# Gate products moved to other stages, packed key weights and a longer turning lag in a two-layer attention trunk

## The chip, the cores and the metric

The kernel runs on one core of a Trainium2 chip. Its engines work beside each other: PE (TensorE, matrix products into PSUM), DVE (VectorE), ACT (ScalarE), POOL (GpSimd), and SP, whose queue here issues every DMA. The metric is the device time of one execution in microseconds (us); lower is better. The outputs must agree with the reference.

## The reference

Two layers of a trunk with 512 latent tokens and 256 context tokens of width 1024. In each layer one input projection feeds two attentions in parallel, a neighbourhood attention (A) and a grouped-query attention (B). Cut to what matters here:

```python
mod_x = jax.nn.silu(c) @ w_ada + b_ada
shift_x, scale_x, gate_x = jnp.split(mod_x[:, None, :], 3, axis=-1)
mod_c = jax.nn.silu(c_ctx) @ w_ada + b_ada
...
hx = _rmsnorm(x, norm_g) * (1.0 + scale_x) + shift_x
px = hx @ w_in
a_k, a_v, b_k, b_v, a_q, b_q, a_z, b_z, g_a, g_b = _split(px, SPLIT_SIZES)
...
a_att = _na_latent(qa, ka, va, cka, cva, rpb, rows)
...
qb = _rope_2d(_rmsnorm(hs(b_q, GQA_Q_HEADS), q_norm_b), pos_row, pos_col)
kb = _rope_2d(_rmsnorm(hs(b_k, GQA_KV_HEADS), k_norm_b), pos_row, pos_col)
b_att = _gqa_latent(qb, k_all, v_all)
out_x = _merge(a_att, b_att, a_z, b_z, g_a, g_b, w_o_a, w_o_b, w_out)
x_new = x + gate_x * out_x
```

`_merge` multiplies each attention by its SiLU path, projects it, weighs it by a sigmoid gate, adds both and projects again. The context tokens go through the same in layer 0; layer 1 needs only their keys and values. So `gate_x` (and `gate_c` in layer 0) is a product of a 1024-vector with the last third of `w_ada`, and it is used only at the end of a layer. It is the *residual gate* of the change.

## The kernel before

**Arithmetic.** Activations and weights are split into a rounded part and the rest (`hi` and `lo`, in fp32r), and each product is three products on PE (`mm3`, lines 346 to 348). A weight tile is loaded (SP) into one of three `raw` buffers, rounded on ACT into `whi`, and the rest is taken on POOL or DVE into `wlo`. `load_w` (line 309) does so one row tile of 128 rows at a time, and `load_w2` (line 323) packs two row tiles of 256 columns into one tile of 512. Both take their tiles from the pool `wp`, with eight `whi` and eight `wlo`, unless `own` names another pool. Token-major products (`tok_proj`) have the activations as weights of PE, channel-major ones (`chan_proj`) the weights.

**Stages of a layer.** First the keys of A (C_AK), values (C_AV) and queries (C_AQ); then A's attention; then keys and values of B (C_BKV) and its queries (C_BQ); then B's attention; then the merge and the output projection. `pipeline` (line 823) runs an attention over eight heads: the scores of head h, the values of head h - 1, and then some pieces of `fill`. The fill is a list of projections that belong to other parts (the SiLU paths, the sigmoid gates, branch A's output projection), in chunks of one weight load and its products; a load stands two chunks ahead of its products. In B's stage `run(fill, 2)` loads the first two chunks after the keys, and `PRE_GQ` pieces run right after the queries. `spread` says over how many heads the fill goes: 9 for A, 8 for B. In B all fill goes through the PSUM tile `psf`.

**Turning.** Keys and queries come token-major. They are normalised (squares on ACT, sums on DVE, the power on POOL), rotated (`rope_heads`, line 463, on DVE and POOL, result `rr`), and transposed on PE to channel-major. The transposes are put off: `to_channels` appends them to `hp["late"]`, and `tok_proj` turns all but the last `hp["lag"]` of them after each token tile. `after_products` (line 381) ties them to PE's place in program order.

**Gate products.** `ada_steps` (line 200) makes a list of steps: a broadcast of the conditioning vector's half into `cb`, and then for each of eight tiles of 128 gate channels a load of 256 KB into `rawb` (two buffers) and one DVE product and sum for the latent vector, in layer 0 a second one for the context vector (line 222, tiles `rawb` and `junk`). Each is tied to DVE's place in program order. There are two halves of the 1024 rows, and `ada_gate` adds them and sends the result out. Before the change the list of both halves runs in B's attention of the same layer: `pipeline` takes `att["per"]` steps after each score tile, two in layer 0 and one in layer 1. With `range(16)` the same helper makes the shifts and scales of layer 1 during layer 0, in the projections and in the output stage; that part stays as it is.

**Order.** The order on every engine's queue is fixed when the program is built. A scheduler follows program order as priority and a simulated timeline for readiness (`schedule_with_timeline_sim=True`), so instructions of neighbouring stages are interleaved. The probability tiles `p` are a ring of `NP_NA` or `NP_GQ` buffers.

Of the kernel before, what the change touches and what calls it, by code (L numbers as in the profile page):

```python
# [26 lines left out]
NP_GQ = (10, 10)  # L27
# [4 lines left out]
PRE_NA, PRE_GQ = 1, 2  # L32
XB, RX = 6, 2
# [14 lines left out]
def hybrid_kernel(es: ExitStack, tc, x, ctx, cvec, w_ada, w_ada0, small, gvec, w_in, w_o_a, w_o_b, w_out,  # L48
# [20 lines left out]
    pm = {}  # L69
# [130 lines left out]
    def ada_steps(l, tiles, halves, nv, pool):  # L200

        cb = {}

        def load(h):
            cb[h] = pool.tile([128, 2, 512], F32, tag="cb", name=nm("cb"), bufs=1)
            for v in range(nv):
                src = cd[8 * v + 4 * h:8 * v + 4 * h + 4].rearrange("k p -> (k p)").unsqueeze(0)
                nc.sync.dma_start(cb[h][:, v, :], src.to_broadcast([128, 512]))

        def load_tile(h, i):  # L210
            cb["w"] = pool.tile([128, 512], F32, tag="rawb", name=nm("rawb"), bufs=2)
            nc.sync.dma_start(cb["w"], w_ada[l, h, i])

        def dot(h, i, v):
            if v == 0:
                load_tile(h, i)
            w = cb["w"]
            o = w if v == nv - 1 else pool.tile([128, 512], BF16, tag="junk", name=nm("junk"), bufs=1)
            ins = nc.cur_bb.bb.instructions
            before = next(j for j in reversed(ins) if j.engine == mybir.EngineType.DVE)  # L220
            n = len(ins)
            V.tensor_tensor_reduce(o, w, cb[h][:, v, :], 1.0, 0.0, ALU.mult, ALU.add, asum[:, i, h, v:v + 1])
            for j in nc.cur_bb.bb.instructions[n:]:
                if j.engine == mybir.EngineType.DVE:
                    tc.add_manual_dep(j, before.name, mybir.DependencyInfo(
                        mybir.DependencyClass.NoSync, mybir.DependencyReason.DATA), reason="program order")
# [81 lines left out]
    def load_w(src, col0, n, nk, lo_eng, k0=0, own=None):  # L308

        pool, x = (wp, "") if own is None else (own, "x")  # L310
        res = []
        for k in range(k0, k0 + nk):
            raw = raw_tile()
            nc.sync.dma_start(raw[:, :n], src[128 * k:128 * k + 128, col0:col0 + n])
            hi = pool.tile([128, 512], F32R, tag="whi" + x, name=nm("whi"), bufs=8)
            S.copy(hi[:, :n], raw[:, :n])  # L316
            lo = pool.tile([128, 512], F32R, tag="wlo" + x, name=nm("wlo"), bufs=8)
# [63 lines left out]
    def after_products(fn):  # L381

        ins = nc.cur_bb.bb.instructions
        n, pe = len(ins), mybir.EngineType.PE
        last = next(i.name for i in ins[::-1] if i.engine == pe)
        fn()
        for i in nc.cur_bb.bb.instructions[n:]:
            if i.engine == pe:
                tc.add_manual_dep(i, last, mybir.DependencyInfo(
                    mybir.DependencyClass.NoSync, mybir.DependencyReason.DATA), reason="program order")  # L390
                last = i.name

    def turn_late(n):

        while len(hp["late"]) > n:
            after_products(hp["late"].pop(0))
# [67 lines left out]
    def rope_heads(npair, ps, rs, ta, tb, dst, t):  # L464
# [4 lines left out]
        r = hp["p"].tile([128, n], F32, tag=f"rr{npair}", name=nm("rr"), bufs=3)  # L469
# [11 lines left out]
    def layer(l, hx, nxt, mid):  # L481
# [5 lines left out]
        W = w_in[l]  # L487
        gq = gcol[:, 48 + 2 * l:49 + 2 * l]
# [114 lines left out]
        else:  # L603
# [4 lines left out]
            bg = []  # L608
# [26 lines left out]
        if True:  # L635
# [127 lines left out]
            def na_scores(h, q, kh, kl):  # L763
                load_bias(h)
                ps_ = []
                for i in range(4):
# [23 lines left out]
                    run(att["bg"], att["per"])  # L790
# [68 lines left out]
            pipeline(fill, 9, na_first, values_of(za, na_values))  # L859
# [7 lines left out]
            cosn = hp["p"].tile([128, 512], F32, tag="sq", name=nm("cosn"), bufs=2)  # L867
# [40 lines left out]
            for t in range(qt):  # L908
                tok_proj(w, 512, a_hx, t, evac_bq)
# [12 lines left out]
            def gq_scores(q, kh, kl):  # L922
                ps_ = []
                for i in range(4):
# [10 lines left out]
                    run(att["bg"], att["per"])  # L935
# [197 lines left out]
```

## Time and profile before

| | us |
|---|---|
| median of 3 runs | 1167.61 (1165.52 to 1169.21) |
| the profiled execution | 1166.55 |
| its span, first to last instruction | 1164.8 |
| granted TensorE clock, mean | 0.997 |

The stages by the trace of the profiled execution: layer 0 starts A's attention at about 140 us, B's keys at 306, B's attention at 375, the merge at 570; layer 1 begins its projections at about 700, A's attention at 780, B's keys at 882, B's attention at 955 and the merge at 1100.

In the profile a line such as "L222 DVE ... rawb<-rawb,cb ... x64 | 53.8, 841" is a group of instructions of one source line, engine and tile: 64 of them, 53.8 us in all, 841 ns on average. Behind the second bar stands the idle time of the engine before them and what ended it. A row of a stretch gives the busy time of each engine in it with the number of instructions, then the granted clock, and DMA's share and rate; for one tile it counts only instructions that write or read this tile. PE's matrix instructions overlap, so their shown durations are longer than the step from one to the next.

### The profile page before, as it was taken

How to read it: one execution, taken by the hardware profiler on the slowest of the kernel's cores; microseconds unless marked ns; L12 is line 12 of the kernel's file. 1: busy time of each engine (PE TensorE's matmuls, PEld its weight loads, DVE VectorE, ACT ScalarE, POOL GpSimd, SP SyncE). 2: the span in 40 equal slices, each digit the busy share in tenths (PEclk: the TensorE clock that was granted, in tenths of full speed). 3: DMA queues.
4: the chain of work that ended last, by engine and by line, in shares of the span. 5: the costliest groups of instructions: out<-in, count | busy, mean ns of one | idle time of the engine just before them, and what ended most of it. 6: DMA issues, size and time to landing. Idle time of an engine off the chain costs nothing.

```text
span 1164.8 us, 17332 instructions
## 1 busy us (share of the span) xinstructions
PE 1127.1 (97%) x6078; PEld 948.9 (81%) x6078; DVE 812.0 (70%) x1512; ACT 574.3 (49%) x1175; POOL 498.0 (43%) x463
## 2 busy tenths in 40 slices
PE   5999999999999999999999999999999999999998
PEld 4688888988988888888788787888888878877686
DVE  4556588876364799798588755349877757898573
ACT  5452266665343555666431355337665445756531
POOL 3362354443275334353411227345544664645311
PEclk9999999999999999999999999999999999999999
DMA  9534212221351343461434423403322525452133
GB/s 372 200 110 136 71 46 65 84 83 63 111 164 47 115 134 100 81 259 37 139 133 123 151 71 92 126 25 107 104 74 66 171 90 182 142 176 91 37 132 95
DMA packets 88129, 134.05 MB, mean 115 GB/s; under 512 B 10757, under 2 KB 52713, under 8 KB 86377
## 3 DMA queue, kind: packets, MB, share of 16 engines
q1 hardware_dynamic: 88040, 132.94, 35.3%
q8 instruction: 48, 0.79, 0.3%
q14 instruction: 41, 0.33, 0.1%
HBM read 115.58 MB, written 17.32 MB: 114 GB/s over the span
## 4 chain that ended last, share of the span: by engine, by line
PE 72%; DVE 10%; POOL 6%; issue 4%; DMA 3%; ACT 2%; SPq 0%; ACTq 0%; POOLq 0%; DVEq 0%
PE psx L348 10%; PE psx L346 10%; PE psx L347 10%; PE psf L346 8%; PE psf L347 8%; PE psf L348 8%; PE pst L654 4%; PE pss L703 2%; PE pss L704 2%; PE pss L780 2%; POOL rsb L255 2%; DVE ptl L658 2%; DMA rawb<-in_w_ada_dram 1%; PE psv L948 1%; DVE mx L930 1%
## 5 line engine op out<-in xcount | busy, mean ns | idle before, releaser
L658 DVE TENSOR_TENSOR ptl<-pst,pth 128x512 fp32r<-128x512 f32 (+1 forms) x176 | 116.1, 671 | 41.0 <-ACT pth L657 40.0
L657 ACT CAST pth<-pst 128x512 fp32r<-128x512 f32 (+1 forms) x176 | 98.9, 576 | 91.7 <-PE pst L654 63.3
L346 PE MATMUL psf<-hx,whi 128*128 128x512 f32 (+1 forms) x368 | 139.4, 379 | 0.0
L347 PE MATMUL psf<-hx,whi 128*128 128x512 f32 (+1 forms) x368 | 138.3, 376 | 0.0
L348 PE MATMUL psf<-hx,wlo 128*128 128x512 f32 (+1 forms) x368 | 138.2, 375 | 0.0
L333 POOL TENSOR_TENSOR wlo<-raw,whi 128x512 fp32r<-128x512 f32 x64 | 91.0, 1425 | 109.9 <-ACT whi L331 96.5
L346 PE MATMUL psx<-whi,hx 128*128 128x512 f32 (+1 forms) x368 | 136.9, 373 | 0.0
L347 PE MATMUL psx<-wlo,hx 128*128 128x512 f32 (+1 forms) x368 | 136.2, 370 | 0.0
L348 PE MATMUL psx<-whi,hx 128*128 128x512 f32 (+1 forms) x368 | 133.8, 370 | 0.0
L319 POOL TENSOR_TENSOR wlo<-raw,whi 128x512 fp32r<-128x512 f32 (+1 forms) x52 | 67.4, 1296 | 149.6 <-ACT whi L316 132.0
L316 ACT CAST whi<-raw 128x512 fp32r<-128x512 f32 (+1 forms) x112 | 65.2, 592 | 112.6 <-PE psx L348 38.3
L331 ACT CAST whi<-raw 128x512 fp32r<-128x512 f32 x128 | 77.6, 621 | 53.2 <-DMA raw<-in_w_in_dram 39.6
L654 PE MATMUL pst<-ident,p 128*128 128x128 f32 x640 | 100.6, 273 | 1.7 <-DVE ptl L658 1.2
L654 PEld LDWEIGHTS pst<-ident,p 128*128 128x128 f32 x640 | 78.1, 141 | 13.7 <-DVE ptl L658 1.0
L644 POOL TENSOR_TENSOR p<-p,r 128x512 f32<-128x512 f32 (+1 forms) x64 | 85.7, 1339 | 5.2
L333 DVE TENSOR_TENSOR wlo<-raw,whi 128x512 fp32r<-128x512 f32 x64 | 62.7, 980 | 31.0 <-ACT whi L331 30.6
L319 DVE TENSOR_TENSOR wlo<-raw,whi 128x512 fp32r<-128x512 f32 (+1 forms) x60 | 48.2, 807 | 45.9 <-ACT whi L316 45.6
L643 POOL TENSOR_SCALAR r<-r 128x1 f32<-128x1 f32 x64 | 21.5, 336 | 137.1 <-DVE r L638 126.6
L346 PEld LDWEIGHTS psx<-whi,hx 128*128 128x128 f32 x368 | 69.8, 190 | 11.9 <-issue 0.8
L348 PEld LDWEIGHTS psf<-hx,wlo 128*128 128x128 f32 x368 | 69.4, 189 | 11.9
L348 PEld LDWEIGHTS psx<-whi,hx 128*128 128x128 f32 x368 | 69.6, 189 | 11.3
L346 PEld LDWEIGHTS psf<-hx,whi 128*128 128x128 f32 x368 | 69.5, 189 | 11.1 <-ACT zt L502 0.3
(239 smaller groups left out, 3065.8 us busy)
## 6 DMA issues: line engine op xcount, KB each, us to landing
raw<-in_w_in_dram SPq DMA_DIRECT2D x160, 256.0 KB, 2.9
rawb<-in_w_ada_dram SPq DMA_DIRECT2D x64, 256.0 KB, 2.7
gs<-zt SPq DMA_DIRECT2D x32, 256.0 KB, 2.4
raw<-in_w_out_dram SPq DMA_DIRECT2D x32, 256.0 KB, 2.8
tg<-gs SPq DMA_DIRECT2D x4, 1536.0 KB, 8.6
rawx<-in_w_ada_dram SPq DMA_DIRECT2D x4, 1024.0 KB, 6.4
rawy<-in_w_ada_dram SPq DMA_DIRECT2D x4, 1024.0 KB, 12.2
raw<-in_w_o_a_dram SPq DMA_DIRECT2D x16, 256.0 KB, 3.3
```

The lines of the kernel that those rows point to most:

```text
L255: G.tensor_tensor(b[:, :w], a[:, :w], ehalf[:, :w], ALU.pow)
L316: S.copy(hi[:, :n], raw[:, :n])
L319: e.tensor_tensor(lo[:, :n], raw[:, :n], F(hi[:, :n]), ALU.subtract)
L331: S.copy(hi, raw)
L333: lo_eng(i).tensor_tensor(lo, raw, F(hi), ALU.subtract)
L346: T.matmul(ps, lhs[0], rhs[0], start=first, stop=False)
L347: T.matmul(ps, lhs[0], rhs[1], start=False, stop=False)
L348: T.matmul(ps, lhs[1], rhs[0], start=False, stop=last)
L644: G.tensor_tensor(p[:, c0:c1], p[:, c0:c1], r[:, i:i + 1].to_broadcast([128, c1 - c0]), ALU.mult)
L654: T.transpose(pt[:, c0:c0 + 128], src, ident)
L657: S.copy(hi[:, n0:n1], pt[:, n0:n1])
L658: V.tensor_tensor(lo[:, n0:n1], pt[:, n0:n1], F(hi[:, n0:n1]), ALU.subtract)
```

## The change

The gate products leave B's attention in part. In layer 0 the first half goes to A's attention, one step a score tile from head 4 on, and the second half stays in B's, one step a score tile. In layer 1 both halves go to the projections of A. B's key and value weights are loaded packed, two row tiles a tile. B's query weights are loaded ahead of B's key products; four of the eight row tiles come from `wp` and four from B's own pool with four buffers. The keys' transposes lag three token tiles instead of two, and the ring of rotated keys has four tiles. The rotation tables of the keys are made first and those of the queries behind the fourth key tile. The cosine tile gets a buffer of its own, and layer 1's B has 11 probability tiles instead of 10. `behind` is `after_products` for any engine.

```diff
-NP_GQ = (10, 10)
+NP_GQ = (10, 11)
...
-    def load_w(src, col0, n, nk, lo_eng, k0=0, own=None):
+    def load_w(src, col0, n, nk, lo_eng, k0=0, own=None, bufs=8):
...
-    def after_products(fn):
+    def behind(engine, fn):
...
-        r = hp["p"].tile([128, n], F32, tag=f"rr{npair}", name=nm("rr"), bufs=3)
+        r = hp["p"].tile([128, n], F32, tag=f"rr{npair}", name=nm("rr"), bufs=4 if npair == 1 else 3)
...
+        nv = 2 if first else 1
+
+        def gate_steps(halves, pool):
+            return (ada_steps(l, range(16, 24), halves, nv, pool)
+                    + ([lambda: ada_gate(l, nv)] if 1 in halves else []))
...
-            bg = []
+            bg = gate_steps((0, 1), hp["p"])
+            run(bg, 1)
         per_bg = -(-len(bg) // (2 + qt))
...
-                    run(att["bg"], att["per"])
+                    run(att["bg"], 1)
...
                 n = len(fill)
-                att["bg"], att["per"] = bg, -(-len(bg) // 30)
                 prev = None
                 for h in range(8):
+                    att["bg"] = bg if h > 3 or pm["n"] == 1 else []
...
-            pipeline(fill, 9, na_first, values_of(za, na_values))
+            bg = gate_steps((0,), att["p"]) if first else []
+            pipeline(fill, 9, na_first, values_of(za, na_values), bg=bg)
...
-            cosn = hp["p"].tile([128, 512], F32, tag="sq", name=nm("cosn"), bufs=2)
+            cosn = hp["p"].tile([128, 512], F32, tag="cosn", name=nm("cosn"), bufs=1)
...
-            for i in range(2):
+
+            def make_tabs(i):
...
+            make_tabs(1)
...
-            w = load_w(W, C_BKV, 256, KT, mix_lo)
+            bg = []
+            w = load_w2(W, C_BKV, KT, mix_lo)
+            w_q = load_w(W, C_BQ, 512, 4, bq_lo) + load_w(W, C_BQ, 512, 4, bq_lo, 4, hp["p"], 4)
+            hp["lag"] = 3
             for t in range(6):
                 tok_proj(w, 256, a_hx, t, evac_bkv)
+                if t == 3:
+                    behind(ON_DVE, lambda: make_tabs(0))
+                run(bg, 1)
+            hp["lag"] = 2
             qbv = big("qb").rearrange("p (j n) -> p j n", j=4)
-            w = load_w(W, C_BQ, 512, KT, bq_lo, own=hp["p"])
...
-                tok_proj(w, 512, a_hx, t, evac_bq)
+                tok_proj(w_q, 512, a_hx, t, evac_bq)
+                run(bg, 2)
...
-            nv = 2 if first else 1
-            bg = ada_steps(l, range(16, 24), (0, 1), nv, att["p"]) + [lambda: ada_gate(l, nv)]
-            run(bg, 1)
+            bg = gate_steps((1,), att["p"]) if first else []
             pipeline(fill, 8, gq_first, values_of(zb, gq_values), early, bg)
```

In the stages of B's keys and queries `bg` is empty, so the two `run(bg, ...)` there do nothing.

More of the change, by code (lines that the diff above doesn't have):

```diff
@@ L32 @@
 PRE_NA, PRE_GQ = 1, 2
+ON_PE, ON_DVE = mybir.EngineType.PE, mybir.EngineType.DVE
 XB, RX = 6, 2
@@ L218, in dot @@
             o = w if v == nv - 1 else pool.tile([128, 512], BF16, tag="junk", name=nm("junk"), bufs=1)
[L219 to L226, printed above, removed]
+            behind(ON_DVE, lambda: V.tensor_tensor_reduce(o, w, cb[h][:, v, :], 1.0, 0.0, ALU.mult, ALU.add,
+                                                          asum[:, i, h, v:v + 1]))
         res = []
@@ L314, in load_w @@
             nc.sync.dma_start(raw[:, :n], src[128 * k:128 * k + 128, col0:col0 + n])
-            hi = pool.tile([128, 512], F32R, tag="whi" + x, name=nm("whi"), bufs=8)
+            hi = pool.tile([128, 512], F32R, tag="whi" + x, name=nm("whi"), bufs=bufs)
             S.copy(hi[:, :n], raw[:, :n])
-            lo = pool.tile([128, 512], F32R, tag="wlo" + x, name=nm("wlo"), bufs=8)
+            lo = pool.tile([128, 512], F32R, tag="wlo" + x, name=nm("wlo"), bufs=bufs)
             e = lo_eng(k)
@@ L379, in hybrid_kernel @@
     hp = {"late": [], "lag": 0}
-    def after_products(fn):
+    def behind(engine, fn):
         ins = nc.cur_bb.bb.instructions
-        n, pe = len(ins), mybir.EngineType.PE
-        last = next(i.name for i in ins[::-1] if i.engine == pe)
+        n = len(ins)
+        last = next(i.name for i in ins[::-1] if i.engine == engine)
         fn()
         for i in nc.cur_bb.bb.instructions[n:]:
-            if i.engine == pe:
+            if i.engine == engine:
                 tc.add_manual_dep(i, last, mybir.DependencyInfo(
@@ L395, in turn_late @@
         while len(hp["late"]) > n:
-            after_products(hp["late"].pop(0))
+            behind(ON_PE, hp["late"].pop(0))
     def run(fill, n):
```

2 lines of the change are left out of this document (1 added, 1 removed).

## The prediction

> **What bounds the kernel now.** I read the profile's first lines, then the busy time of each engine by stage, then, for the stages that the change touches, the same table for single tiles.
>
> ```profile
> PE 1127.1 (97%) x6078; PEld 948.9 (81%) x6078; DVE 812.0 (70%) x1512; ACT 574.3 (49%) x1175; POOL 498.0 (43%) x463
> ```
>
> PE is busy for 1127.1 of 1164.8 us. The change takes no product from PE, so it can give only time that PE now loses: 37.7 us that show as idle, and some more inside the modelled ends. Where that lies, stage by stage:
>
> ```profile
> core 0: us, PE busy (x) PEld busy (x) DVE busy (x) ACT busy (x) POOL busy (x), PEclk, DMA share, GB/s
> 80.00:140.00 60.00, 60.00 (x280) 49.47 (x280) 38.78 (x88) 15.95 (x27) 21.73 (x19) 1.00 0.35 106
> 140.00:225.00 85.00, 85.00 (x529) 75.89 (x528) 71.21 (x142) 54.80 (x117) 43.18 (x38) 1.00 0.21 63
> 225.00:300.00 75.00, 75.00 (x475) 67.06 (x474) 49.65 (x107) 42.41 (x100) 26.62 (x30) 1.00 0.21 69
> 390.00:475.00 85.00, 83.69 (x500) 72.64 (x498) 79.49 (x157) 47.64 (x103) 31.85 (x28) 1.00 0.36 115
> 475.00:580.00 105.00, 100.75 (x616) 87.38 (x615) 77.80 (x133) 59.22 (x120) 51.04 (x42) 1.00 0.39 124
> 700.00:780.00 80.00, 78.93 (x366) 64.67 (x365) 34.68 (x52) 35.20 (x64) 38.80 (x34) 1.00 0.28 85
> 880.00:898.00 18.00, 16.57 (x114) 13.91 (x113) 12.22 (x28) 11.22 (x24) 5.86 (x7) 1.00 0.20 63
> 920.00:955.00 35.00, 31.69 (x145) 25.16 (x144) 19.66 (x24) 13.37 (x25) 23.75 (x18) 1.00 0.30 92
> 955.00:1035.00 80.00, 78.63 (x396) 65.26 (x396) 65.16 (x119) 47.94 (x93) 40.70 (x33) 1.00 0.60 195
> 1035.00:1060.00 25.00, 25.00 (x135) 21.00 (x134) 21.06 (x35) 16.22 (x32) 10.10 (x10) 1.00 0.29 85
> 1060.00:1100.00 40.00, 36.16 (x190) 26.79 (x189) 28.23 (x47) 24.12 (x47) 18.41 (x18) 1.00 0.12 41
> ```
>
> In order: projections of layer 0 (80 to 140); its first attention (140 to 225 early heads, 225 to 300 late heads); its second attention (390 to 475, with the gate products, and 475 to 580); projections of layer 1 (700 to 780); the end of its first attention (880 to 898); the queries of its second (920 to 955); that attention itself (from 955). The late part of layer 0's first attention leaves DVE idle for a third, while the start of its second keeps DVE busy for 79.49 of 85 and PE loses 1.31. Layer 1 loses 3.31 in 920 to 955, 1.37 in 955 to 1035 and at least 3.84 in 1060 to 1100.
>
> How much that last stretch really loses I count. First the steps from start to start of queued PE instructions:
>
> ```profile
> 301.17 0.40 PE L346 MATMUL psf<-hx,whi 128*128 128x512 f32 x1
> 301.40 0.39 PE L347 MATMUL psf<-hx,whi 128*128 128x512 f32 x1
> ...
> 891.03 0.27 PE L652 MATMUL pst<-ident,p 128*128 128x128 f32 x1
> 891.14 0.49 PE L654 MATMUL pst<-ident,p 128*128 128x128 f32 x3
> ```
>
> So a 512-wide product takes 0.23 and a transpose 0.11, whatever their shown durations. Next, for the same stretch, the rows of the tiles psf, pst, psv, pss and psx in this order:
>
> ```profile
> 1060.00:1100.00 40.00, 3.60 (x12) 1.71 (x10) 0.66 (x1) 0.00 (x0) 1.00 0.12 41
> ...
> 1060.00:1100.00 40.00, 13.11 (x88) 10.75 (x88) 14.91 (x23) 12.70 (x22) 1.00 0.12 41
> ...
> 1060.00:1100.00 40.00, 18.71 (x48) 8.65 (x48) 2.74 (x4) 2.32 (x4) 1.00 0.12 41
> ...
> 1060.00:1100.00 40.00, 5.38 (x24) 4.02 (x24) 5.66 (x6) 6.15 (x14) 1.00 0.12 41
> ...
> 1060.00:1100.00 40.00, 3.99 (x18) 3.48 (x19) 0.00 (x0) 0.00 (x0) 1.00 0.12 41
> ```
>
> 88 transposes x 0.11 + 102 products x 0.23 = 33.2, so 6.8 of the 40 us are lost. Only 12 of these products are fill (psf): the projections that are put between attention steps have run out, and PE follows DVE and ACT. The attention's progress is the DVE count of tile ptl, six a head:
>
> ```profile
> 955.00:1035.00 80.00, 6.69 (x16) 3.02 (x16) 10.71 (x16) 1.00 0.60 195
> 1035.00:1060.00 25.00, 3.16 (x8) 1.51 (x8) 6.89 (x10) 1.00 0.29 85
> 1060.00:1100.00 40.00, 10.75 (x24) 4.50 (x24) 14.91 (x23) 1.00 0.12 41
> ```
>
> When the fill ends at 1060, 26 of 49 are done (48, and one counted at a border). **The attention lags its fill**, and the gate products (lines 222) stand in DVE in the part where it falls behind.
>
> **The change part by part.**
>
> ```profile
> L222 DVE CUSTOM_DVE_ANT_0 rawb<-rawb,cb 128x512 f32<-128x512 f32 x64 | 53.8, 841 | 1.5 <-DMA rawb<-in_w_ada_dram 0.8
> L222 DVE CUSTOM_DVE_ANT_0 junk<-rawb,cb 128x512 bf16<-128x512 f32 x48 | 37.0, 772 | 9.9 <-DMA rawb<-in_w_ada_dram 9.6
> ...
> L222 DVE DVE_READ_ACCUMULATOR2_ANT asum<- 128x1 f32 x112 | 9.0, 80 | 0.0
> ```
>
> *Layer 1's gate products leave its second attention.* 16 x (0.841 + 0.080) = 14.7 us of DVE, 16 loads and two broadcasts go. Without them DVE needs 65.16 - 14.7 + 21.06 + 28.23 = 99.75 for 49 steps, 2.04 each, so 14.7 us are worth 7.2 steps. At the fill's end 33 instead of 26 would be done; the tail shrinks from 23 steps to 16, and its 6.8 with it: -2.1. Of the 1.37 before it I take half: -0.7. Together **-2.8**. Bounds: 0 if DVE does not pace the attention (it is at 81%, not full), -8.2 if the fill then lasts to the end.
>
> *They go to layer 1's projections*, 16 products in six tile steps. DVE there has 34.68 of 80, with them 49.4, or 62%. The nearest row is layer 0's same stage, 80 to 140, which holds 32 such products at 38.78 of 60 (65%) with PE busy for 60.00 of 60.00. Cost **0**; cover gone, 14.7.
>
> ```profile
> SPq L212 <- DVE asum L222: 105.0, 48, 11.6
> ...
> PE pst L422 <- DVE rr L477: 4.1, 7, 1.4
> ```
>
> Their loads pass SP, where a load waits for one of two buffers, up to 11.6 us, with the weights of the next projection behind it. In layer 0 that happened under a full PE too, so it stays at nothing. The gate sum and its small transfer come some 300 us before their use.
>
> *Layer 0's first half goes from the second attention to heads 4 to 7 of the first.* It takes 8 x (0.841 + 0.772) + 16 x 0.080 = 14.2 from DVE. In 390 to 475 DVE falls from 94% to 77%, and I give back the idle time of that stretch: **-1.3**; bounds 0 and -3.4, the last if half of the 4.25 lost in 475 to 580 goes as well. The second half now comes one step a score tile, through five heads. At its new place DVE rises from 49.65 to 63.9 of 75, 85%. The nearest row, 140 to 225, has 84% and no PE idle, so **0**. The other bound is the bare end of layer 1's first attention, where fill is gone: by the share of weight loads in a full stretch (67.06 of 75) the 13.91 there are 15.6 us of work in 18, so +2.4. Eight loads and two broadcasts stand there before bias loads and weights in SP; the same cover holds.
>
> *Packing, early query weights, third lag.*
>
> ```profile
> raw<-in_w_in_dram SPq DMA_DIRECT2D x160, 256.0 KB, 2.9
> ...
> raw<-in_w_in_dram SPq DMA_DIRECT2D x16, 128.0 KB, 2.1
> ```
>
> Eight 128 KB transfers a layer become four of 256 KB: 16.8 us of landings become 11.6, and the casts halve in number and double in width. PE does the previous stage meanwhile: nothing, and at most 5.2 a layer gained. The slots matter more. Four of eight query weight pairs now use the shared eight, and keep them until the last query product. So only the first of the two prefetched fill chunks can load during the queries. Layer 1 shows what the second one does there now, in the chain of waits, on ACT, and on PE:
>
> ```profile
> 918.03 4.69 DMA raw<-in_w_in_dram
> ...
> 922.75 0.62 ACT whi L331
> ```
> ```profile
> 922.75 1.25 ACT L331 CAST whi<-raw 128x512 fp32r<-128x512 f32 x2 [2.47 <-DMA raw<-in_w_in_dram]
> 923.90 0.60 ACT L404 ACTIVATE sq<-psf 128x512 f32<-128x512 f32 x1
> ...
> 932.47 0.63 PE L422 MATMUL pst<-ident,rr 128*128 128x128 f32 x4 [1.41 <-DVE rr L477]
> ```
>
> The squares of the first query tile queue on ACT behind a cast that waits for a fill weight, and at the end PE waits 1.41 for the rotated queries. Of the 4.1 in seven such waits of both layers I take this one and 0.1 of the keys' own: **-1.5**. Bounds: -4.1, and the second chunk too late, which is a rival. Next late is then POOL's chain for the later query tiles, at 23.75 of 35. The eleventh probability tile lets scores run one tile further ahead and the two later tables take two DVE instructions off the front: nothing.
>
> Sum: -2.8 + 0 - 1.3 + 0 - 1.5 = **-5.6** on the profiled execution's 1166.55 (span 1164.8 and 1.75 around it), or 1160.95. The median of the runs, 1167.61, stands 1.06 higher; I add half to every case: **1161.5**.
>
> [...]
>
> ```profile
> L222 DVE CUSTOM_DVE_ANT_0 rawb<-rawb,cb x64: 667/691/1889, 92.5 to 1030.4; 128x512 f32<-128x512 f32 x64
> ```
>
> Some of them take 1.889 where the median is 0.691, so they meet something. If each of the 16 in layer 1 held POOL's chain of the norms by 0.69, and PE with it, that were +11.0. [...]
>
> **The rivals.**
>
> *More: the fill lasts.* The whole 6.8 and 1.37 of layer 1, 3.4 of layer 0 and the 1.5 go: -13.1, 1154.0. For it: PE loses nothing in 1035 to 1060, where fill is there. Against it: the last head's values come behind all fill.
>
> *Nothing but the queries.* The order on each engine is set when the program is built, and already puts query weights and fill early. If the attention is paced by the chain of PE, ACT and DVE and not by DVE's sum, only -1.5 is left: 1165.6. For it: DVE at 81% in 955 to 1035; against it: 94% in layer 0.
>
> *Slower: the second fill chunk is late.* It cannot load before the last query product.
>
> ```profile
> L331 ACT CAST whi<-raw 128x512 fp32r<-128x512 f32 x128 | 77.6, 621 | 53.2 <-DMA raw<-in_w_in_dram 39.6 <-PE psf L347 4.8 <-PE psx L347 3.5
> ...
> L333 POOL TENSOR_TENSOR wlo<-raw,whi 128x512 fp32r<-128x512 f32 x64 | 91.0, 1425 | 109.9 <-ACT whi L331 96.5 <-PE psx L347 10.1 <-PE psf L347 2.6
> ```
>
> One tile takes 2.9 + 0.62 + 1.43 = 4.95, four in a row 19.8. Against it stand the first chunk's products, 48 x 0.23 = 11.0 in layer 1, and half as much again, 16.5, in layer 0. If nothing overlaps, PE waits 8.8 and 3.3, and the query gain is gone: -4.1 + 12.1 = +8.0, 1175.1. It decides once the four take over 11.0 together; with three buffers they should overlap to some 9.
>
> *Slower: POOL held by the moved products*, as above: -5.6 + 11.0, 1172.5.
>
> **How the numbers follow.** The forecast gets 0.50, more gain 0.15, the queries alone 0.20, the late chunk 0.10, POOL held 0.03; 0.02 is for what I don't see. About 0.3%, 3.5 us, can be told from no change here, so faster means under 1164.1. The forecast (own range 1158.5 to 1164.5) puts 0.48 there, the larger gain 0.15 and the queries alone 0.02: 0.65. Within: 0.22, mostly the queries alone. Slower: 0.13. The range goes from just below the larger gain, 1153.5, to 1170, and leaves out the two slower cases.
>
> **What would show it.** Right: no line-222 work after 955; the ptl count before the fill's end in layer 1 over 30; PE in the last 40 us before its merge above 36.16; DVE in the first 85 us of layer 0's second attention near 65 and PE full; PE still full in late layer 0 heads; no wait of over 1 us for rotated queries in layer 1. Wrong: the tail keeps its 23 steps (DVE did not pace it), PE waits for fill weights right after the queries (slots), or layer 0's first attention ends bare.

## The result and the profile after

The changed kernel takes 1155.68 us (median of 4 runs, 1154.87 to 1157.16) against 1166.57 for the kernel before, run beside it (4 runs, 1165.51 to 1169.21). The ratio is 0.9905, 95% interval 0.9883 to 0.9926, so it is 11.1 us faster, give or take 2.5. The forecast's sum was 5.6. The profiled execution has a span of 1153.4 against 1164.8.

The first row of the page of after, busy time of each engine, and the table by stage, cut at the borders that correspond to those of before (columns as there):

```profile
PE 1123.0 (97%) x6078; PEld 949.0 (82%) x6078; DVE 809.8 (70%) x1508; ACT 573.9 (50%) x1167; POOL 495.0 (43%) x459
```

```profile
80.00:140.00 60.00, 60.00 (x281) 49.44 (x280) 38.87 (x88) 15.93 (x27) 21.21 (x20) 1.00 0.37 106
225.00:300.00 75.00, 74.65 (x471) 66.60 (x470) 59.85 (x137) 42.23 (x98) 31.83 (x30) 1.00 0.34 103
389.00:474.00 85.00, 84.78 (x516) 74.75 (x516) 65.54 (x126) 48.87 (x104) 30.66 (x28) 1.00 0.27 87
474.00:570.00 96.00, 91.70 (x562) 79.17 (x561) 73.71 (x125) 56.61 (x115) 46.07 (x39) 1.00 0.36 107
700.00:776.00 76.00, 75.25 (x350) 61.59 (x349) 41.24 (x84) 32.57 (x56) 38.70 (x34) 1.00 0.49 137
876.00:894.00 18.00, 16.54 (x111) 13.83 (x110) 13.85 (x30) 11.36 (x24) 6.34 (x7) 1.00 0.23 64
916.00:946.00 30.00, 30.00 (x141) 24.58 (x140) 20.42 (x22) 13.38 (x24) 23.88 (x18) 1.00 0.33 101
946.00:1026.00 80.00, 80.00 (x412) 66.99 (x411) 58.32 (x92) 53.11 (x103) 38.05 (x35) 1.00 0.38 130
1048.00:1088.00 40.00, 37.23 (x194) 28.62 (x193) 28.02 (x44) 22.55 (x42) 17.05 (x15) 1.00 0.18 54
```

The reader is to see four things. Layer 1's queries (916 to 946) now keep PE full, where 920 to 955 before had 31.69 of 35. The attention behind them (946 to 1026) has PE full too, and its last 40 us hold 37.23 against 36.16. The start of layer 0's second attention (389 to 474) has DVE at 65.54 of 85, where it had 79.49, and PE at 84.78 against 83.69. Layer 0's late first heads (225 to 300) took the gate products and lose 0.35.

PE issues the same 6078 matrix instructions in both kernels, so the gain must be time that PE lost between them. I count it by stage: from the start of each PE instruction to the start of the next, less the step of a queued one (0.228 and 0.120 us for 512 and 256 columns, the usual steps inside the stretches where PE is full, and 0.082 for 128, the mean over a burst of three transposes, whose steps are 0.109, 0.109 and 0.028). A stage reaches from its attention's first query split (tile `qs` on DVE) to its last head's output (`ho`), or from that to the next `qs`. This is my own sum over the trace's rows. Its level hangs on the steps taken, its differences hardly do. One trace of each kernel stands behind it, and traces scatter: in `e1_gates`, `e2_gates_l1` and `e7_defer`, experiments below that leave the order of ScalarE in this stage as before has it, layer 1's keys and queries lose 4.3, 5.4 and 4.2, so that the 5.4 of before stands at the upper end and some 1 us in this row is no effect of the change.

| lost by PE, us | before | after |
|---|---|---|
| layer 0: up to its first attention | 18.0 | 18.3 |
| layer 0: first attention | 6.2 | 6.7 |
| layer 0: keys and queries of the second | 2.7 | 1.3 |
| layer 0: second attention | 17.2 | 15.1 |
| layer 0's output and layer 1's projections | 5.5 | 4.8 |
| layer 1: first attention | 9.4 | 9.4 |
| layer 1: keys and queries of the second | 5.4 | 1.0 |
| layer 1: second attention | 17.0 | 13.6 |
| layer 1: output | -0.4 | -0.4 |
| sum | 81.1 | 69.7 |

The difference, 11.4, is the whole difference of the spans. The keys' and queries' stages of both layers give 5.8 of it, the two second attentions 5.5.

### The profile page after: what moved, and what is told of

Read it like the earlier page. It is cut to its first block, busy times and chain, and to the rows that moved or that the text cites. A ratio compares the mean times of both kernels' runs of the same rounds, so it can differ in the third digit from the quotient of the medians.

```text
span 1153.4 us, 17280 instructions
## 1 busy us (share of the span) xinstructions
PE 1123.0 (97%) x6078; PEld 949.0 (82%) x6078; DVE 809.8 (70%) x1508; ACT 573.9 (50%) x1167; POOL 495.0 (43%) x459
## 4 chain that ended last, share of the span: by engine, by line
PE 83%; DVE 7%; issue 3%; POOL 2%; ACT 2%; DMA 2%; ACTq 0%; POOLq 0%; DVEq 0%
PE psx L341 12%; PE psx L343 12%; PE psx L342 12%; PE psf L341 9%; PE psf L342 9%; PE psf L343 9%; PE pst L655 5%; PE pss L704 2%; PE pss L705 2%; PE psv L959 2%; PE psv L958 1%; PE pss L781 1%; PE pst L417 1%; DVE wlo L328 1%; DVE ptl L659 1%
## 5 line engine op out<-in xcount | busy, mean ns | idle before, releaser
L328 POOL TENSOR_TENSOR wlo<-raw,whi 128x512 fp32r<-128x512 f32 x68 | 95.0, 1402 | 108.9 <-ACT whi L326 87.8
L314 POOL TENSOR_TENSOR wlo<-raw,whi 128x512 fp32r<-128x512 f32 x44 | 60.4, 1373 | 140.4 <-ACT whi L311 123.8
L311 ACT CAST whi<-raw 128x512 fp32r<-128x512 f32 x96 | 58.7, 623 | 103.5 <-PE psx L343 38.6
L326 ACT CAST whi<-raw 128x512 fp32r<-128x512 f32 x136 | 82.5, 622 | 50.3 <-DMA raw<-in_w_in_dram 34.1
L328 DVE TENSOR_TENSOR wlo<-raw,whi 128x512 fp32r<-128x512 f32 x68 | 70.2, 1033 | 28.3 <-ACT whi L326 27.8
L342 PEld LDWEIGHTS psx<-wlo,hx 128*128 128x128 f32 x368 | 69.6, 189 | 11.0
```

Source lines behind the costliest of these rows:

```text
L326: S.copy(hi, raw)
L328: lo_eng(i).tensor_tensor(lo, raw, F(hi), ALU.subtract)
L342: T.matmul(ps, lhs[0], rhs[1], start=False, stop=False)
```

## The experiments

All ratios are to the kernel before, run beside the kernel, with 95% intervals.

### The gate products alone

`e1_gates` is before with all moves of the gate products, `e2_gates_l1` with those of layer 1 alone. Both have `gate_steps` and the new place in layer 1's projections; the first also has `run(att["bg"], 1)` and the new place in layer 0's first attention. In the second:

```diff
-            bg = []
+            bg = gate_steps((0, 1), hp["p"])
+            run(bg, 1)
         per_bg = -(-len(bg) // (2 + qt))
...
-            bg = ada_steps(l, range(16, 24), (0, 1), nv, att["p"]) + [lambda: ada_gate(l, nv)]
+            bg = gate_steps((0, 1), att["p"]) if first else []
```

> The kernel before with only the gate products moved (both layers). By the recorded reasons: -2.8 in layer 1's second attention and -1.3 in layer 0's, so -4.1 us against the kernel before, ratio 0.9965. By a second reading, from the two traces (unbroken steps of PE counted stage by stage): some -5.5, ratio 0.995. By the rival that DVE does not pace the attention: 0, ratio 1.000. If layer 0's first attention ends bare, its late heads lose PE time.

> The kernel before with only layer 1's gate products moved to its projections; layer 0's stay. By the recorded reasons -2.8 us, ratio 0.9976, with the ptl count at the fill's end near 33; by the second reading -3.4, ratio 0.997; by the rival 0.

Measured: all moves 1161.78, ratio 0.9960 (0.9947 to 0.9973), layer 1's alone 1163.46, 0.9981 (0.9972 to 0.9989). So layer 1's move is worth about 2.2 us by the ratio, and layer 0's 2.4 more by the ratios or 1.7 by the medians; the intervals are about as wide as that difference. The count agrees: in `e2_gates_l1` layer 1's second attention loses 14.5 instead of 17.0, in `e1_gates` layer 0's loses 14.9 instead of 17.2 and its first attention 6.8 instead of 6.2. Layer 1's second attention of `e2_gates_l1`, all tiles (the first stretch is 955 to 1035, as before):

```profile
955.00:1035.00 80.00, 79.88 (x409) 66.76 (x408) 57.84 (x90) 52.52 (x103) 37.19 (x34) 1.00 0.39 132
1060.00:1100.00 40.00, 36.52 (x188) 27.43 (x187) 24.82 (x40) 23.00 (x43) 17.43 (x16) 1.00 0.13 41
```

Before, the same stretches had PE at 78.63 and 36.16 and DVE at 65.16. The DVE count of the tile ptl, which says how far the attention has come when its fill ends, goes from 26 steps of 48 before to 30 in both kernels. What the prediction said of the gate products holds in mechanism and roughly in size.

### The keys' and queries' stage alone, and what of it is needed

`e3_keys` is the change without the moves of the gate products and with 10 probability tiles. It has the packing, the query weights loaded ahead of the key products and split over two sets of slots, the longer lag, the fourth `rr` tile, the cosine tile's own buffer and the later tables. From there parts are taken back. `e4_keys_own8` gives all eight query weight pairs slots of their own, and `e5_keys_small` keeps the split; both have lag 2, three `rr` tiles and the cosine tile in its old buffer. `e6_keys_late` is `e3_keys` with the loads behind the key products in program order. `e4_keys_own8` differs from `e3_keys` in these lines, besides the `rr` tiles and the cosine tile:

```diff
-            w_q = load_w(W, C_BQ, 512, 4, bq_lo) + load_w(W, C_BQ, 512, 4, bq_lo, 4, hp["p"], 4)
-            hp["lag"] = 3
+            w_q = load_w(W, C_BQ, 512, KT, bq_lo, own=hp["p"])
...
-            hp["lag"] = 2
```

> The changed kernel with the gate products put back where they were and 10 probability tiles: only the stage of the second attention's keys and queries is changed. By the recorded reasons -1.5 us, ratio 0.9987. By the second reading, that this term was undersized, -5.5, ratio 0.9953, most of it in layer 1 between its first and second attention.

> As e3_keys, but all eight query weight pairs in the stage's own pool, so that the second fill chunk can load during the queries again (for its room the cosine tile shares a buffer as before, three tiles of rotated keys, lag 2). Slots theory (the gain is that the second chunk's casts no longer stand ahead of the query squares on ACT): at most -2 us, ratio over 0.998, with PE waiting over 1 us for rotated queries in layer 1. Early-weights theory (the gain comes from the query weights' place): the same as e3_keys within 1 us. Lag theory (three tiles against two): over 1 us slower than e3_keys, with waits at the keys' transposes.

> The same as e4_keys_own8 but with the four and four split of the change: it differs from e4 only in the slots. Slots theory: some 3 to 4 us faster than e4, ratio 0.996 to the kernel before. Early-weights theory: equal to e4. Lag theory: equal to e4, both slower than e3_keys.

> As e3_keys, but the query weights (four and four) are loaded after the keys' products in program order, as before. Early-weights theory: loses most of e3's gain, ratio over 0.998. Slots theory: keeps it, within 1 us of e3_keys.

Measured: `e3_keys` 1161.62, 0.9963 (0.9951 to 0.9975); `e4_keys_own8` 1163.39, 0.9973 (0.9963 to 0.9983); `e5_keys_small` 1161.41, 0.9959 (0.9947 to 0.9972); `e6_keys_late` 1162.13, 0.9975 (0.9966 to 0.9984). The stage alone is worth 4.3, not 1.5. Without lag, fourth tile and cosine buffer it is worth as much, so these do nothing that can be measured. The place of the loads in program order does not show in layer 1's stage either: it loses 1.0 in `e3_keys`, `e5_keys_small` and `e6_keys_late` alike, though 3.0 in `e4_keys_own8`. (The time of `e6_keys_late` gains less than that of `e3_keys`, 2.9 against 4.3, but the intervals overlap, and what the count shows of it is 0.3 in layer 1's second attention.) The slots matter, though less than all of the gain: 1.6 lie between `e4_keys_own8` and `e5_keys_small`, which differ in nothing else, and 3.1 are left without the split, more than the 1.6 that the packing gives alone (next section). So without the split the early place may be worth something. In both comparisons the intervals overlap.

Why shows in ScalarE's and GpSimd's timelines of layer 1 (start, duration, and behind the shape the idle time before it). First before: the square of the first key tile, one of the casts behind it, and GpSimd's first and last instruction for the query tiles:

```profile
898.39 0.27 ACT L404 ACTIVATE sq<-psf 128x128 f32<-128x128 f32 x1
...
911.37 0.62 ACT L316 CAST whi<-raw 128x512 fp32r<-128x512 f32 x1 [2.14 <-DMA raw<-in_w_in_dram]
```
```profile
925.45 0.57 POOL L253 TENSOR_SCALAR rsa<-ss 128x8 f32<-128x8 f32 x1
...
948.17 1.29 POOL L474 TENSOR_TENSOR ry<-ry,tabs 128x512 f32<-128x512 f32 x1 [1.60 <-DVE rr L472]
```

Then `e5_keys_small`, the same instructions:

```profile
898.33 0.27 ACT L399 ACTIVATE sq<-psf 128x128 f32<-128x128 f32 x1
...
916.53 0.60 ACT L399 ACTIVATE sq<-psf 128x512 f32<-128x512 f32 x1 [0.47 <-PE psf L343]
```
```profile
917.94 0.25 POOL L248 TENSOR_SCALAR rsa<-ss 128x8 f32<-128x8 f32 x1 [3.09 <-DVE ss L401]
...
940.87 1.67 POOL L469 TENSOR_TENSOR ry<-ry,tabs 128x512 f32<-128x512 f32 x1 [0.62 <-PE psx L342]
```

Before, the first query square stood behind a cast that waited: PE's last product for it (`psf`) starts at 917.62 and takes 0.39, but ScalarE takes the square only at 923.90, behind fill casts from 922.75 on, ahead of which it stands idle for 2.47 until the weight has landed. In all, 15 weight casts stand in ScalarE's order there between the first attention's last head and the first query square: 8 of query weights and 7 of fill, several of them waiting for a landing (2.14 in the row above, 2.47 and 1.15 in others). The normalisation of the four query tiles on GpSimd, some 24 us from its first to its last instruction, starts behind the square and ends with PE's waits for rotated queries. In `e5_keys_small` there are 8 such casts, the square waits only 0.47 for the products themselves, and GpSimd starts at 917.94 instead of 925.45. The four shared slots do this: four query tiles are cast before the first attention ends, and as they hold the slots the second fill chunk finds no place ahead of the first three query squares (its casts come at 929 to 935). The number of casts is not all of it: in `e4_keys_own8` also 15 stand there, and the square comes 3.6 us earlier than before, as its casts wait less for landings (0.40 for the fourth, where before has 4.04).

### Packing alone, and the second fill chunk out of the way

Four kernels take other ways to the same square. `e10_pack` is before with the packed load alone. `e7_defer` issues the second fill chunk behind the query products in program order. `e9_act_tie` also ties its casts to their place in ScalarE's order, and `e11_pack_act` is that with the packing.

```diff
-            w = load_w(W, C_BKV, 256, KT, mix_lo)
+            w = load_w2(W, C_BKV, KT, mix_lo)
...
-            run(fill, 2)
+            run(fill, 1)
...
             zb = big("zb")
+            behind(mybir.EngineType.Activation, lambda: run(fill, 1))
```

> The kernel before with the keys' weights packed and nothing else. Queue theory: the casts ahead of the first query squares stay eight, so under 1 us, ratio 1.000 to 0.999. Loading theory: the fill's first chunk finds free slots earlier, -2 us, ratio 0.998.

> The kernel before with one line moved: the second fill chunk's load stands behind the query products of the second attention instead of ahead of them; no packing, no lag, no other place of the query weights, gate products as before. Slots theory: -3 to -4 us, ratio 0.997 or less, no wait of over 1 us for rotated queries in layer 1. Early-weights and lag theory: 0.

> The kernel before, with the casts of the second fill chunk tied behind the last query squares in ACT's built order (in e7 that order came out as before). Nothing else changes. Queue theory (query squares stand behind casts that wait for fill weights): -2 to -3 us, ratio 0.998, the first query squares of layer 1 some 3 us earlier after the stage's start, its wait gone. Loading theory (the stage is late because 16 weight tiles and the keys' eight half tiles load one after the other): 0.

> e9 and e10 together: packed keys, and the second chunk's casts behind the query squares. If these two make up the gain of e3_keys, -4.4 us, ratio 0.996; if the early place of the query weights or the table order is needed too, the PE loss of layer 1's stage stays over 2 us against 1.0 in e3.

Measured: `e10_pack` 1164.06, 0.9986 (0.9977 to 0.9995); `e7_defer` 1165.78, 1.0003 (0.9994 to 1.0012); `e9_act_tie` 1164.65, 0.9999 (0.9990 to 1.0008); `e11_pack_act` 1164.91, 0.9993 (0.9985 to 1.0002). Packing alone gives about 1.6, and by the count it lies in layer 0, whose keys and queries lose 1.3 as in after, where before has 2.7. `e7_defer` says nothing about the queue: the scheduler drew the loads forward again, and ScalarE's order in this stretch is that of before. The two ties remove the waits for rotated queries all but 0.3 and 0.4 us, but the time does not move, since a new wait stands in their place. PE's longest waits in `e9_act_tie`, then the end of its query stage on ScalarE and PE's first scores:

```profile
PE pss L715 <- DVE qs L709: 2.7, 1, 2.7
```
```profile
951.19 0.62 ACT L331 CAST whi<-raw 128x512 fp32r<-128x512 f32 x1 [1.99 <-DMA raw<-in_w_in_dram]
951.71 0.59 ACT L514 ACTIVATE zt<-psx 128x512 f32<-128x512 f32 x1
952.76 0.62 ACT L331 CAST whi<-raw 128x512 fp32r<-128x512 f32 x1 [0.45 <-DMA raw<-in_w_in_dram]
953.28 0.58 ACT L448 COPY qb<-pst 128x512 f32<-128x512 f32 x1
```
```profile
955.28 0.79 PE L715 MATMUL pss<-gk,qs 128*128 128x512 f32 x1 [2.71 <-DVE qs L709]
```

The copy of the last query tile now queues behind the late chunk's casts, and the first scores wait 2.71 for it. That is the mechanism of the rival "the second fill chunk is late", at 2.7 instead of the 12.1 that it was priced at, and through ScalarE's queue instead of missing weights. `e11_pack_act` has the same wait at 2.4. In `e9_act_tie` the granted clock of PE is 0.50 in the 3.39 us behind it (last section). In both kernels the attention's first part loses 2.8 by the count, where before has 1.2. The change itself does not have it: after has no such wait.

### The packing and the slots, and which of the slots' two effects

> Before with the keys' weights packed two row tiles a tile and the query weights split four in the shared slots, four in slots of their own; loaded where before loads them; tables, lag 2 and everything else as before. Queue theory: what counts is how many weight casts stand in ScalarE's order between the last head of the first attention and the first query square. Here these are 8, as in e5_keys_small, against 16 before, so the first query square comes near 916 in layer 1, the stage loses 1.0 instead of 5.4, and the time falls by 4.4, ratio 0.996. Rival, the early place of the loads or the order of the tables matters: only the packing's gain of e10_pack stays, 1.6, ratio 0.9986, with the waits for rotated queries kept.

> As e5_keys_small, but the first four query weight tiles are cast only after ScalarE's work of the first key tile; they still hold the shared slots, so the second fill chunk still waits for them. It tells apart what the four slots do. If the early casts count: 12 casts (8 query, 4 fill) stand ahead of the first query square, which comes near 920 in layer 1; the stage loses about 3, the gain over before falls to 2.5 to 3, ratio 0.9976, and waits for rotated queries come back. If only the absence of the second chunk's four casts counts: square near 916, loss 1.0, gain 4.4 as in e5_keys_small, ratio 0.996.

```diff
-            w = load_w(W, C_BQ, 512, KT, bq_lo, own=hp["p"])
+            w = load_w(W, C_BQ, 512, 4, bq_lo) + load_w(W, C_BQ, 512, 4, bq_lo, 4, hp["p"], 4)
```

That line and the packed load, with the parameter `bufs` that the line needs, are all of `e13_pack_split`. `e14_no_preload` is `e5_keys_small` with the loads behind the first key tile:

```diff
             for t in range(6):
                 tok_proj(w, 256, a_hx, t, evac_bkv)
+                if t == 0:
+                    w_q = []
+                    behind(mybir.EngineType.Activation, lambda: w_q.extend(load_w(W, C_BQ, 512, 4, bq_lo)))
+                    w_q += load_w(W, C_BQ, 512, 4, bq_lo, 4, hp["p"], 4)
```

Measured: `e13_pack_split` 1161.15, 0.9961 (0.9948 to 0.9973); `e14_no_preload` 1161.96, 0.9963 (0.9951 to 0.9975). Two edited lines carry the whole gain of the stage. In `e14_no_preload` the first query square comes late, as it would if the early casts counted:

```profile
898.03 0.28 ACT L399 ACTIVATE sq<-psf 128x128 f32<-128x128 f32 x1
...
919.89 0.61 ACT L399 ACTIVATE sq<-psf 128x512 f32<-128x512 f32 x1
```

but the stage loses only 1.6 and the time is that of `e5_keys_small` within the intervals. Some waits for `rr` come back, 0.48 in layer 1 and 1.01 at a key tile of layer 0, whose stage loses 2.4 where `e5_keys_small` loses 1.3. So keeping the second fill chunk out gives most of it, and the early casts some 0.6 in layer 1 and 1.1 in layer 0 by the count, which the times don't settle. All kernels side by side, by the two squares and the loss of layer 1's stage:

| kernel | first key square to first query square, us | stage loses, us |
|---|---|---|
| e2_gates_l1 | 25.6 | 5.4 |
| before | 25.5 | 5.4 |
| e1_gates | 24.8 | 4.3 |
| e7_defer | 24.7 | 4.2 |
| e10_pack | 24.6 | 4.1 |
| e9_act_tie | 22.6 | 5.0, of it 2.9 at the first scores |
| e11_pack_act | 22.2 | 4.3, of it 2.6 at the first scores |
| e4_keys_own8 | 21.9 | 3.0 |
| e14_no_preload | 21.9 | 1.6 |
| e6_keys_late | 19.7 | 1.0 |
| after | 19.5 | 1.0 |
| e8_np10 | 19.5 | 0.9 |
| e13_pack_split | 19.3 | 0.9 |
| e5_keys_small | 18.2 | 1.0 |
| e3_keys | 18.1 | 1.0 |
| e12_keep | 18.1 | 1.0 |

Up to about 20 us the delay is hidden; beyond that PE loses part of it. Above 24 us the loss follows the delay about one for one, and it does so in the wait for the first query tile, 1.41 before and 0.42 in `e1_gates`. The wait for the last tile is 1.32 or 1.33 in both:

```profile
930.09 0.63 PE L422 MATMUL pst<-ident,rr 128*128 128x128 f32 x4 [0.42 <-DVE rr L477]
...
949.02 0.63 PE L422 MATMUL pst<-ident,rr 128*128 128x128 f32 x4 [1.33 <-DVE rr L477]
```

Equal delays of 21.9 cost 3.0 and 1.6, so the first square is not everything. Most of that difference is the wait for the last tile, still 1.32 in `e4_keys_own8` and 0.48 in `e14_no_preload`. In the first, three of the second chunk's four casts stand ahead of the first query square and one right behind it; in the second all four stand behind the third square. Why the last wait is shorter there no run shows by itself.

### The eleventh tile, and fill kept to the end

`e8_np10` is after with `NP_GQ = (10, 10)`. `e12_keep` is after with the last pieces of the fill kept behind the last head's values:

```diff
                 if last is not None:
-                    run(fill, len(fill))
+                    run(fill, len(fill) - 2 * len(spans))
                     last()
...
-            pipeline(fill, 8, gq_first, values_of(zb, gq_values), early, bg)
+            pipeline(fill, 9, gq_first, values_of(zb, gq_values), early, bg)
```

> The changed kernel with 10 probability tiles in layer 1's second attention, as before. By the recorded reasons the same time as the changed kernel, 1155.7 within 1 us, ratio 0.9905. If the eleventh tile lets the attention run ahead of the fill, up to 2 us slower than that.

> The changed kernel, with spread 9 instead of 8 in the second attention and the last two fill pieces (four in layer 0) held back until behind the last head's values. If the tail is bare because fill stands ahead of the last head in program order, -2 to -4 us against the changed kernel, ratio 0.988; if the fill runs early whatever its place because attention steps are not ready, 0.

Measured: `e8_np10` 1156.20, 0.9920 (0.9906 to 0.9933), which overlaps the 0.9905 of after. Its trace has 30 steps of ptl ahead of the fill's end where after has 32, and 14.3 lost in layer 1's second attention against 13.6, so the eleventh tile may be worth 0.7; the times don't settle it. The kernel with 10 tiles is also the sum of the two parts: `e1_gates` and `e3_keys` alone gave 4.7 and 4.3 by their ratios, together 9.0, and `e8_np10` gives 9.3. `e12_keep` 1166.12, 1.0005 (0.9997 to 1.0014): the whole gain is gone. Layer 0's second attention loses 22.8 instead of 15.1, 9.0 of it in these 20 us:

```profile
495.00:500.00 5.00, 2.14 (x14) 1.62 (x13) 4.01 (x5) 4.93 (x10) 5.00 (x3) 1.00 0.90 322
500.00:505.00 5.00, 4.41 (x24) 3.43 (x23) 4.87 (x6) 1.83 (x6) 4.92 (x5) 1.00 0.99 393
505.00:510.00 5.00, 2.61 (x12) 2.07 (x12) 4.94 (x8) 2.15 (x4) 3.11 (x3) 0.88 1.05 428
510.00:515.00 5.00, 5.00 (x27) 4.55 (x27) 1.85 (x5) 1.63 (x4) 0.00 (x0) 0.78 0.87 354
```

GpSimd is full for the first 10 us, and its timeline shows with what: branch A's four splits (`gal`), 8 us in one piece.

```profile
494.46 7.97 POOL L544 TENSOR_TENSOR gal<-za,gah 128x768 fp32r<-128x768 f32 x4
...
504.65 1.26 POOL L669 TENSOR_TENSOR zb<-zb,ho 64x512 f32<-64x512 f32 x1
```

A head's product (`zb`) comes behind them, and ScalarE's copy of the next head at 505.94 waits 4.08 for it. But PE's longest wait is recorded for VectorE, and the chain of work ahead of it lies on VectorE from 496.62 on. PE's row, then two rows of VectorE's timeline:

```profile
506.72 0.66 PE L655 MATMUL pst<-ident,p 128*128 128x128 f32 x4 [2.31 <-DVE ptl L659]
```
```profile
503.48 2.59 DVE L642 TENSOR_SCALAR p<-p,r 128x256 f32<-128x256 f32 x2
505.99 0.68 DVE L659 TENSOR_TENSOR ptl<-pst,pth 128x512 fp32r<-128x512 f32 x1
```

VectorE is busy for 13.82 of the 15 us from 495 to 510, and some of its instructions take longer than their like in after (the two `p` above 2.59 against 1.10). After has the same four splits, at another point of the attention:

```profile
488.87 8.00 POOL L544 TENSOR_TENSOR gal<-za,gah 128x768 fp32r<-128x768 f32 x4
```

Whether GpSimd's piece lengthens VectorE's instructions no run shows. In layer 1 the edit did not keep the fill back: its last product comes with 28 of 48 steps of ptl done, where after has 32, and the attention loses 16.4 instead of 13.6. So this edit did not test whether more fill in the tail would help. That question stays open.

## Why the prediction was right in sign and half the size

**The gate products leave layer 1's second attention, -2.8.** Right. No gate product runs there any more; line 220 in the list of one line's instructions (duration minimum, median and maximum in ns, then first and last start) ends in layer 1's projections:

```profile
L220 DVE CUSTOM_DVE_ANT_0 rawb<-rawb,cb x64: 673/686/1781, 92.8 to 765.8; 128x512 f32<-128x512 f32 x64
```

Alone it gave 2.2 by the times and 2.5 by the count. The ptl count, forecast at 33, is 30 with this edit alone and 32 in after:

```profile
946.00:1060.20 114.20, 12.02 (x30) 5.66 (x30) 21.75 (x32) 1.00 0.34 114
1060.20:1088.00 27.80, 8.09 (x18) 3.37 (x18) 10.94 (x16) 1.00 0.19 58
```

(The last fill product of the attention stands at 1060.2; 32 are done by then and 16 left, as many as forecast.) DVE did pace the attention, though each step freed bought somewhat less than the sum over DVE said.

**They go to layer 1's projections, 0.** Right: PE has 75.25 of 76 there with DVE at 41.24, and the stage loses 4.8 against 5.5.

**Layer 0's first half, -1.3, and 0 at its new place.** Right, within what can be told: 1.7 to 2.4 between the two gate kernels. DVE fell to 65.54 in the first 85 us, as forecast (near 65), the attention lost 2.3 less, and the price at the new place was 0.6, between the 0 taken and the 2.4 of the other bound: PE lost 0.35 in 225 to 300.

**"Packing, early query weights, third lag", -1.5.** This is the step that failed. It read: "Of the 4.1 in seven such waits of both layers I take this one and 0.1 of the keys' own." The mechanism was the right one for the slots, the squares that queue on ScalarE behind a cast waiting for a fill weight, and that the shared slots keep the second chunk out was in the prediction too. The size was not: the stage alone measured -4.3, the bound of -4.1 that was set aside, and by the count 5.8 in the change, some 1 of which is the scatter of traces. The waits were priced one by one, as if only the wait for the first query tile hung on that square. The prediction's own table has PE idle for 3.31 in 920 to 955; these are the waits at the other three tiles, beside the 1.41 that it shows:

```profile
939.47 0.63 PE L422 MATMUL pst<-ident,rr 128*128 128x128 f32 x4 [0.41 <-DVE rr L477]
...
944.87 0.63 PE L422 MATMUL pst<-ident,rr 128*128 128x128 f32 x4 [0.18 <-DVE rr L477]
...
951.39 0.63 PE L422 MATMUL pst<-ident,rr 128*128 128x128 f32 x4 [1.32 <-DVE rr L477]
```

It took POOL's chain as the next thing to be late and left these standing. But all four query tiles pass GpSimd in order behind the first square, and the chain still takes some 24 us: it begins earlier. When the square comes 6 to 7 us earlier, the waits go together. After's list of PE's waits has no wait of `pst` for `rr` any more, where before had 4.1. (From start to start each of the seven cost some 0.16 more than its idle time, 1.57 for the 1.41, which is 1.1 of what the stages gave beyond 4.1.) One term under that heading was put at nothing and is not: the packing gives about 1.6 alone, in layer 0 by the count. The split of the slots gives the rest, in layer 1. Lag, fourth tile and tables were worth nothing measurable, nor was the early place where the split stands.

**The sum and the rivals.** With -4.3 in that place the sum is -8.4, and the eleventh tile's 0.7, if it is real, makes it -9.1, inside the measured 8.6 to 13.7. What of the middle value, 11.1, lies beyond it no run assigns. The time lies 1.7 above the rival "More: the fill lasts", but not by that mechanism: the tail is still there. In the last 40 us, counted as in the prediction (rows of psf, psv, pss, psx and pst),

```profile
1048.00:1088.00 40.00, 11.49 (x43) 7.28 (x41) 2.02 (x3) 0.00 (x0) 1.00 0.18 54
...
1048.00:1088.00 40.00, 16.58 (x44) 7.81 (x44) 2.74 (x4) 2.32 (x4) 1.00 0.18 54
...
1048.00:1088.00 40.00, 2.58 (x12) 1.96 (x12) 4.65 (x5) 4.75 (x10) 1.00 0.18 54
...
1048.00:1088.00 40.00, 3.42 (x15) 3.00 (x16) 0.00 (x0) 0.00 (x0) 1.00 0.18 54
...
1048.00:1088.00 40.00, 12.10 (x80) 9.81 (x80) 14.98 (x22) 11.72 (x20) 1.00 0.18 54
```

114 products x 0.23 + 80 transposes x 0.11 = 35.0, so 5.0 are lost where 6.8 were. (Both are low: 0.11 is the step inside a burst of transposes, and with the mean of 0.082 it is 7.2 against 9.3.) The rival "POOL held by the moved products" found nothing: GpSimd has 38.70 in layer 1's projections, 38.80 before, and PE lost no more. That each of these products holds GpSimd's chain for 0.69 us, from which the +11.0 came, was the author's assumption, and no run shows it: the stage of layer 0's output and layer 1's projections lost 4.8 after and 5.5 before. The longest of the products still takes 1.781 against a median of 0.686 us, at no price for PE here; what it meets no run shows.

## What to carry to other kernels

One late instruction in ScalarE's queue delayed a whole chain here (the first query square came at 923.90 before and at 916.53 in `e5_keys_small`): price an edit in such a queue by when the first link starts and how much of that delay is hidden (here some 20 of 25.5 us), not by picking among the waits recorded at the chain's end. A load drawn ahead of need has a price when its cast waits in such a queue, and a limit on slots held it back better than its place in program order or a tie to a later place, which only moved the wait (layer 1's stage loses 0.9 in `e13_pack_split`, 4.2 in `e7_defer` and 4.3 in `e11_pack_act`). When work is moved, look which engine's queue it now stands in and what is due behind it: in `e9_act_tie` the last query copy stood behind the casts that had been moved out of the squares' way, and the first scores waited 2.71 for it.

## What was not expected of the hardware

Two pauses of PE, one in `e12_keep` and one in `e9_act_tie`, were paid twice: by the wait, and by a granted clock of 0.50 behind it. In `e12_keep` PE was busy for 9.16 of the 15 us from 495 to 510, and the granted clock, 1.00 in the stretches of the tables above, is 0.88 from 505 to 510 and 0.78 from 510 to 515 (rows above). In finer stretches it is 0.50 for 3.39 us, behind 3.39 us in which PE was busy for 1.36 and never idle for more than 2.31 at a time; in a stretch of 3.38 us with 1.82 shortly before it is 1.00. In `e9_act_tie` the same comes behind the wait of 2.71. The rows of `e12_keep`, then those of `e9_act_tie`:

```profile
495.12:498.50 3.38, 1.82 (x12) 1.29 (x10) 2.58 (x2) 3.33 (x7) 3.38 (x3) 1.00 0.90 298
505.36:508.75 3.39, 1.36 (x7) 1.02 (x8) 3.33 (x6) 1.14 (x3) 2.63 (x3) 1.00 1.09 457
508.77:512.16 3.39, 3.39 (x16) 3.18 (x15) 1.85 (x4) 0.99 (x2) 0.10 (x1) 0.50 1.02 418
```
```profile
951.82:955.21 3.39, 0.76 (x4) 0.29 (x2) 1.36 (x2) 2.86 (x6) 1.27 (x1) 1.00 0.66 214
955.23:958.62 3.39, 3.34 (x10) 2.85 (x11) 2.01 (x3) 1.20 (x2) 0.00 (x0) 0.50 0.69 158
```

PE's timeline of `e12_keep` shows the instructions queued without a gap there:

```profile
509.57 0.41 PE L342 MATMUL psf<-gal,whi 128*128 128x256 f32 x1
509.78 0.41 PE L343 MATMUL psf<-gah,wlo 128*128 128x256 f32 x1
```

The same products in after's timeline:

```profile
499.51 0.28 PE L343 MATMUL psf<-gah,wlo 128*128 128x256 f32 x1
499.63 0.28 PE L341 MATMUL psf<-gah,whi 128*128 128x256 f32 x1
```

They start 0.21 apart in the one and 0.12 in the other. Twelve such products cost 1.1 us beyond the idle time itself. What sets the granted clock no run shows.
